# Last output projections of the second attention and of the state space layer, token tile by token tile

## The chip, the cores and the metric

The kernel runs on one core of one Trainium2 chip. The metric is device time in microseconds (us) of one execution; the time of a kernel is the median of its runs. Engines are named as the profile names them: PE (TensorE matmuls), PEld (its weight loads), DVE (VectorE), ACT (ScalarE), POOL (GpSimd), SP (SyncE, which issues most of the DMAs).

## The reference

One sequence of 512 tokens with 1024 features goes through two blocks, all in float32. The first block mixes a gated convolution, a stick-breaking attention and a cross attention to a memory, and ends in a feed-forward layer. The second block is what the change touches:

```
for layer in range(2):
    h = rmsnorm(x, norm_mix[layer])
    mix = attn_layer(h, ...) if layer % 2 == 0 else ssm_layer(h, ...)
    x = x + mix
    h = rmsnorm(x, norm_ffn[layer])
    x = x + conv_ffn(h, ...)        # (silu(causal_dwconv(gate)) * up) @ w_out

attn_layer: ... return concatenate([oa, ob], -1) @ w_out          # 1024 x 1024
ssm_layer:  ... y = rmsnorm of groups of 512 features (yg)
            return y @ w_out                                     # 2048 x 1024
```

The last projection of `attn_layer` takes the 512 features of the heads of kind a (rows 0 to 511 of its `w_out`); the last one of `ssm_layer` takes the 512 features of group 3 (rows 1536 to 2047).

## The kernel before

**Precision by halves.** Every float32 product is made of three fast matmuls (`mm3`): both operands are split into a high part (rounded to fp32r) and a low part (the rest), and high x high, high x low and low x high are accumulated in one PSUM bank. So an operand is ready only when ACT has cast its high part and DVE has subtracted to get the low part. Weights come from HBM into two raw buffers, and go through chunks of 128 x 512 (`whi` by ACT, `wlo` by DVE), nine of which there is room for (`WB`). Activations go through `Feat.put` (L431), which casts (`hh`, `oTh`, `yTh`) and subtracts (`hl`, `oTl`, `yTl`).

**Jobs.** The program is a list of jobs, each a block of weights with a generator `run` that records PE's matmuls. `run_jobs` (L355) records one job after the other; at each `yield` it splits further weight chunks, as far as there is room, and lets other tasks take a step: attention units, state space units, norms. Those tasks sit in a heap ordered by the planner's own clock `now`; `until(...)` lets tasks run until what the job needs has been recorded. The result is one fixed order of instructions on each engine, and each engine works strictly through its own.

**The places in question.** `jobB` is a projection from features to tokens: for each of four token tiles of 128 tokens it accumulates over its weight chunks into one bank (`gb` in the profile), 3 matmuls of 128 x 512 for each of 4 chunks, so 12 for a tile and half. It gives 512 of the 1024 output features; the two halves of the features are two jobs, half 0 for all four tiles and then half 1 for all four. `residual` adds the bank to the residual stream `x` on DVE and, when it is the last such sum, calls the hook of the next norm (`normer`). The hook records for that tile and half: ACT squares the row and sums it (`junk`), and later PE transposes the tile (`tr`), DVE multiplies by the gain (`xg`), ACT casts (`hh`) and DVE subtracts (`hl`). When both halves of a tile are there, the row's scale follows (`rs`).

In the state space layer, `outp(3, True)` is the last projection. Its `pre` waits until all four token tiles of group 3 are recorded (`(g, 3) in S`), where each tile is: PE products `y1` and `y2`, on DVE a join of four rows (`y`, `yo`, `y`, `y`), a square on ACT (`yj`), a power on POOL (`yr`), a scaling on DVE, four transposes on PE (`yT`), and the cast and the difference (`yTh`, `yTl`). In the second attention, the last two jobs use the heads of kind a (`oT`), whose tiles come from a pipeline of units that is still running.

After either place comes a convolutional feed-forward layer. Its first job (`jobA` with `between`) takes features 0 to 511 of all tokens for both of its feature tiles, then features 512 to 1023; `between` then makes a row of all tokens' scales (`R`), which the gated convolution (`fg`, `fy` on DVE) needs.

Of the kernel before, what the change touches and what calls it, by code (L numbers as in the profile page):

```python
# [19 lines left out]
NT = 4  # L20
# [36 lines left out]
class Job:  # L57
    def __init__(self, pieces, nk, nc, run, pre=None):
        self.pieces = pieces
        self.nk = nk  # L60
        self.nc = nc
        self.run = run
        self.pre = pre
        self.speed = 0.6
        self.source = None
        self.after = None
        self.prefetch = None
        self.ahead = None


@with_exitstack
def kernel(ctx: ExitStack, tc: tile.TileContext, ins: dict, out: bass.AP, parts=(1, 2, 3, 4, 5)):
# [59 lines left out]
    def spawn(gen, delay=0.0):  # L132
        count[0] += 1
        heapq.heappush(tasks, (now[0] + delay, count[0], gen))

    def step():

        ready, n, gen = heapq.heappop(tasks)
        now[0] = max(now[0], ready)
        outer, done[0] = done[0], 0.0  # L140
        try:
            d = next(gen)
        except StopIteration:
            done[0] = outer
            return
        d, lag = d if isinstance(d, tuple) else (d or 0.0, LAG)
        heapq.heappush(tasks, (max(now[0] + d, done[0] + lag), n, gen))
        done[0] = outer
# [10 lines left out]
    quota = [2]  # L159
# [3 lines left out]
    def room(tag, n=1):  # L163

        for k, v in freed.items():
            live[k] -= sum(t <= now[0] for t in v)
            freed[k] = [t for t in v if t > now[0]]
        if tag == "g":
            return live["g"] + live["t"] + n <= BANKS
        return live["t"] + n <= BANKS - max(quota[0], live["g"])  # L170

    def bank(tag, nm="p"):

        while not room(tag):
            soon = [t for k in ("g", "t") for t in freed[k]]
            if tag == "g" and soon:
                now[0] = min(soon)
            else:
                until(lambda: room(tag))
        live[tag] += 1  # L180
        return pp.tile([128, 512], F32, tag="ps", name=nm, bufs=BANKS)

    def rel(tag):
        freed[tag].append(max(done[0], now[0]))

    def hand_over():

        live["g"] -= 1
        live["t"] += 1
# [51 lines left out]
    def pump():  # L241
        while tasks and tasks[0][0] <= now[0]:
            step()

    def drain():
        while tasks:
            step()

    def until(ready):

        limit = now[0] + 500.0
        while not ready():
            if tasks:
                step()
            else:
                now[0] += 0.1
            assert now[0] < limit
# [5 lines left out]
    class Flow:  # L263
# [19 lines left out]
        def run(self, units):  # L283

            while units:
                while self.count - self.at[-1] >= self.cap:
                    yield 0.3
                spawn(self.stages(self.count, units.pop(0)))
                self.count += 1
                yield self.every  # L290


    jobs = []
    raws = {}
    split = {}
# [38 lines left out]
    def split_lo():  # L334
        while late:
            late.pop(0)()
# [18 lines left out]
    def run_jobs():  # L355
        chunks = [(i, c) for i, j in enumerate(jobs) for c in range(max(1, j.nk * j.nc // 512))]
        st = {"n": 0, "used": 0}

        def more(limit, upto=None):
            while limit > 0 and st["n"] < len(chunks):  # L360
                i, c = chunks[st["n"]]
                if upto is not None and i > upto:
                    return
                if upto is None and st["used"] - freed_chunks[0] >= WB:
                    return
                split_lo()
                split_hi(i, c)
                st["n"] += 1
                st["used"] += 1
                limit -= 1  # L370

        for i, j in enumerate(jobs):
            if j.pre is not None:
                j.pre()
            more(99, i)
            if late and chunks[st["n"] - 1][0] == i:
                split_lo()
            sp_ = 0.5
            for _ in j.run(W(i)):
                split_lo()  # L380
                sp_ += j.speed
                if sp_ >= 1:
                    more(1)
                    sp_ -= 1
                pump()
            st["used"] -= len(split.pop(i))
            freed_chunks[0] = 0
        drain()

    def mm3(ps, sh, sl, mh, ml, first, last):  # L390
        pe.matmul(ps, lhsT=sh, rhs=mh, start=first, stop=False)
        pe.matmul(ps, lhsT=sh, rhs=ml, start=False, stop=False)
        pe.matmul(ps, lhsT=sl, rhs=mh, start=False, stop=last)

    class Feat:
# [25 lines left out]
        def ready(self, k, a, b):  # L421
            return all((k, t) in self.got for t in range(a, b, 128))
# [84 lines left out]
    def jobB(wap, r0, nk, c0, X, k0, state, first, last, evac, ntt=NT, width=512, pre=None):  # L507

        def run(w):
            x = X()  # L510
            quota[0] = ntt if first and not last else 2
            for tt in range(ntt):
                if first:
                    state[tt] = bank("g", "gb")
                ps = state[tt][:, 0:width]
                for k in range(nk):
                    wh, wl = w.get(k, 0, width)
                    xh, xl = x.rd(k0 + k, tt * 128, tt * 128 + 128)
                    mm3(ps, xh, xl, wh, wl, first and k == 0, last and k == nk - 1)
                    if k % 2 and k + 1 < nk:  # L520
                        yield
                if last:
                    hand_over()
                    if not evac(tt, ps):
                        rel("t")
                yield

        jobs.append(Job([(0, width, wap[r0:r0 + nk * 128, c0:c0 + width])], nk, width, run, pre))
        if ntt < NT:
            jobs[-1].speed = 1  # L530

    def projB(wap, r0, nk, c0, X, evac, ntt=NT, pre=None, k0=0, cut=None, mid=None):
        state = {}
        n = 0
        for m in cut or [4] * (nk // 4):
            jobB(wap, r0 + n * 128, m, c0, X, k0 + n, state, n == 0, n + m == nk, evac, ntt, 512,
                 pre if n == 0 else mid)
            n += m

# [13 lines left out]
    def scaled_add(ps, scale, tt, half):  # L555

        xa = x_half(tt, half)
        dve.scalar_tensor_tensor(out=xa, in0=ps, scalar=scale[:, tt:tt + 1], in1=xa, op0=ALU.mult, op1=ALU.add)
# [182 lines left out]
    hooks = {}  # L741
# [4 lines left out]
    def x_half(tt, h):  # L746
        return x_ap(tt)[:, h * 512:(h + 1) * 512]
# [5 lines left out]
    def x_done(tt, h):  # L753

        hooks["x"](tt, h)
# [68 lines left out]
    def residual(c, last=True, scale=None):  # L824

        def evac(tt, ps):
            xa = x_half(tt, c)
            if scale:
                scaled_add(ps, scale(), tt, c)
            else:  # L830
                dve.tensor_add(xa, ps, xa)
            if last:
                x_done(tt, c)
        return evac
# [4 lines left out]
    def first_block():  # L839
# [140 lines left out]
        for half in range(2):  # L980
            projB(ins["w_mem_kv"], 0, KD, half * 512, lambda: M["m"], k_evac(half), ntt=2)
        for half in range(2):
            projB(ins["w_mem_kv"], 0, KD, D + half * 512, lambda: M["m"], v_evac(half), ntt=2)
# [328 lines left out]
    def attn(G):  # L1312
        w = ins["attn_w_in_2"]
        S = {}
# [178 lines left out]
        X = lambda: G["h"]  # L1493
# [23 lines left out]
        wo = ins["attn_w_out_2"]  # L1517
        O = lambda: oT["o"]
        for half in range(2):
            jobB(wo, 512, 4, half * 512, O, 4, {}, True, True, residual(half, False), pre=va_end)  # L1520
        for half in range(2):
            jobB(wo, 0, 4, half * 512, O, 0, {}, True, True, residual(half),
                 pre=(lambda: hooks.update(x=hooks["next2"])) if half == 0 else None)

# [73 lines left out]
    def ssm(G):  # L1600
        w = ins["ssm_w_in_2"]
        wo = ins["ssm_w_out_2"]
        X = lambda: G["h"]
        S = {}
# [288 lines left out]

        def outp(g, last):
            def pre():
                until(lambda: (g, 3) in S)
                if last:
                    hooks.update(x=hooks["next4"])
            for half in range(2):
                projB(wo, g * 512, 4, half * 512, lambda: S["yT", g], residual(half, last),  # L1900
                      pre=pre if half == 0 else None)

        group(0)
        for g in range(1, 4):
            group(g)
            outp(g - 1, False)
        outp(3, True)


# [110 lines left out]
```

## Time and profile before

| | |
|---|---|
| median of 3 runs | 2476.68 us (2473.72 to 2478.02) |
| profiled execution, its own time | 2474.39 us |
| span of that execution in the trace | 2472.7 us, 30712 instructions |
| PE busy | 2432.4 us (98%) |
| DVE busy | 1527.4 us (62%) |
| ACT busy | 1113.9 us (45%) |
| POOL busy | 215.0 us (9%) |
| granted TensorE clock, mean | 0.998 |

The span is the time from the first to the last instruction; 1.7 us lie around it. Matmuls overlap: one of 128 x 512 has a duration of 0.39 us, but the next starts 0.23 us after it. So PE's busy share does not tell how much of its time is lost; gaps between starts do. In the timeline a bracket at a row's end gives the idle time of the engine just before it and the engine and tile that ended it.

### The profile page before, as it was taken

What the parts mean: (1) busy time and instruction counts of PE and PEld (TensorE: products, weight loads), DVE (VectorE), ACT (ScalarE), POOL (GpSimd) and SP (SyncE); (2) the same over time, 40 slices, a digit from 0 to 9 for tenths busy, and PEclk for the clock granted to TensorE, in tenths of its full rate; (3) what the DMA queues carried; (4) which work ended last, traced back from release to release, by engine and by line L of the source; (5) the groups of instructions that cost most, each with busy time, mean ns of one, the idle gap of its engine ahead of it and who ended that gap; (6) DMA issues with size and microseconds to landing.
All of it is one profiled execution on the core that took longest, in us unless ns stands there. A gap on an engine that the chain in (4) does not pass through costs nothing.

```text
span 2472.7 us, 30712 instructions
## 1 busy us (share of the span) xinstructions
PE 2432.4 (98%) x11556; PEld 1975.4 (80%) x11556; DVE 1527.4 (62%) x2808; ACT 1113.9 (45%) x2406; POOL 215.0 (9%) x279
## 2 busy tenths in 40 slices
PE   8999999999999999999998999999999999999999
PEld 6877877788888888888776888888778887888887
DVE  6436466653434566656756666776698687667674
ACT  6545444432333445545666333333565635433332
POOL 1102011101110011102100000000000000001010
PEclk9999999999999999999999999999999999999999
DMA  5323332333323565622221354442432431345442
GB/s 208 103 59 95 111 100 80 88 109 111 99 89 119 153 163 144 120 91 82 68 87 35 104 143 120 131 107 80 118 107 77 124 115 60 97 142 119 137 111 77
DMA packets 218533, 264.78 MB, mean 107 GB/s; under 512 B 7024, under 2 KB 157936, under 8 KB 218384
## 3 DMA queue, kind: packets, MB, share of 16 engines
q1 hardware_dynamic: 198848, 222.83, 27.8%
q0 software_dynamic: 15232, 29.36, 7.4%
q10 hardware_dynamic: 4304, 10.62, 1.5%
q8 instruction: 91, 1.49, 0.3%
q14 instruction: 58, 0.48, 0.1%
HBM read 254.33 MB, written 4.26 MB: 105 GB/s over the span
## 4 chain that ended last, share of the span: by engine, by line
PE 87%; DVE 6%; issue 4%; ACT 1%; DMA 1%; POOL 0%; ACTq 0%; SPq 0%; POOLq 0%; DVEq 0%
PE ga L87 47%; PE gb L87 21%; PE gw L87 11%; PE y L87 1%; PE as L87 1%; DVE wlo L120 1%; DVE fy L120 1%; PE o L87 1%; PE tr L92 1%; PE aT L92 1%; PE z L87 1%; PE ao L87 1%; PE ap L92 1%; DVE ae L120 0%; DVE y L120 0%
## 5 line engine op out<-in xcount | busy, mean ns | idle before, releaser
L87 PE MATMUL ga<-hh,whi 128*128 128x512 f32 x1672 | 661.4, 396 | 0.0
L87 PE MATMUL ga<-hh,wlo 128*128 128x512 f32 x1672 | 651.8, 390 | 0.3 <-DVE wlo L120 0.2
L87 PE MATMUL ga<-hl,whi 128*128 128x512 f32 x1672 | 651.3, 390 | 0.0
L120 DVE TENSOR_TENSOR wlo<-raw,whi 128x512 fp32r<-128x512 f32 x701 | 479.3, 704 | 227.6 <-ACT whi L120 226.5
L120 ACT CAST whi<-raw 128x512 fp32r<-128x512 f32 x701 | 412.8, 617 | 156.8 <-PE ga L87 62.5
L87 PEld LDWEIGHTS ga<-hh,wlo 128*128 128x128 f32 x1672 | 313.2, 187 | 67.7 <-DVE wlo L120 1.2
L87 PEld LDWEIGHTS ga<-hh,whi 128*128 128x128 f32 x1672 | 313.4, 187 | 66.3 <-issue 3.0
L87 PEld LDWEIGHTS ga<-hl,whi 128*128 128x128 f32 x1672 | 313.6, 188 | 64.9 <-issue 1.7
L87 PE MATMUL gb<-whi,hh 128*128 128x512 f32 (+1 forms) x416 | 171.6, 412 | 0.0
L87 PE MATMUL gb<-wlo,hh 128*128 128x512 f32 (+1 forms) x416 | 159.3, 383 | 2.3 <-DVE wlo L120 2.2
L87 PE MATMUL gb<-whi,hl 128*128 128x512 f32 (+1 forms) x416 | 159.8, 384 | 0.0
L120 DVE TENSOR_TENSOR wlo<-b,whi 128x512 fp32r<-128x512 f32 x196 | 131.2, 686 | 36.9 <-ACT whi L120 36.9
L120 ACT ACTIVATE fy<-fy,cols 128x512 f32<-128x512 f32 x60 | 43.5, 726 | 202.1 <-DVE fy L120 200.4
L120 ACT CAST whi<-b 128x512 fp32r<-128x512 f32 x196 | 114.1, 616 | 15.6 <-PE gw L87 11.2
L120 DVE SCALAR_TENSOR_TENSOR x<-gw,rsp,x 128x512 f32<-128x512 f32 x98 | 70.0, 750 | 69.3 <-PE gw L87 69.2
L120 DVE SCALAR_TENSOR_TENSOR fy<-fg,cols,fy 128x510 f32<-128x510 f32 (+1 forms) x136 | 102.1, 751 | 4.8
L120 DVE TENSOR_TENSOR fg<-ga,R 128x512 f32<-128x512 f32 x68 | 46.9, 690 | 78.6 <-PE ga L87 67.2
L87 PEld LDWEIGHTS gb<-wlo,hh 128*128 128x128 f32 x416 | 78.6, 189 | 17.6 <-DVE wlo L120 3.7
L87 PEld LDWEIGHTS gb<-whi,hl 128*128 128x128 f32 x416 | 78.2, 188 | 16.0
L87 PEld LDWEIGHTS gb<-whi,hh 128*128 128x128 f32 x416 | 78.4, 188 | 14.6 <-issue 1.7
L655 POOL DMA_DIRECT2D b<-in_ffn_w_out_dram x32 | 38.5, 1205 | 507.6 <-DVE wlo L120 503.6
L87 PE MATMUL gw<-whi,fss 128*128 128x512 f32 x256 | 81.4, 389 | 0.0
(316 smaller groups left out, 3958.7 us busy)
## 6 DMA issues: line engine op xcount, KB each, us to landing
raw<-in_ffn_w_in_dram SPq DMA_DIRECT2D x44, 1024.0 KB, 5.1
raw<-in_w_in_dram SPq DMA_DIRECT2D x32, 1024.0 KB, 5.0
raw<-in_w_up_dram SPq DMA_DIRECT2D x16, 1024.0 KB, 5.4
b<-in_ffn_w_out_dram POOLq DMA_DIRECT2D x32, 512.0 KB, 5.7
raw<-in_ssm_w_in_dram SPq DMA_DIRECT2D x16, 1024.0 KB, 5.3
b<-in_w_down_dram POOLq DMA_DIRECT2D x24, 512.0 KB, 6.0
b<-in_ffn_w_out_dram SPq DMA_DIRECT2D x12, 1024.0 KB, 7.6
b<-in_w_down_dram SPq DMA_DIRECT2D x9, 1024.0 KB, 7.7
```

The lines of the kernel that those rows point to most:

```text
L87: nc.tensor.matmul(o, lhsT=lhsT, rhs=rhs, **kw)
L92: nc.tensor.transpose(o, i, idn)
L120: return fn(*args, **kw)
L655: nc.gpsimd.dma_start(out=r3(R[nm][:, a * 512:(c + 1) * 512], c + 1 - a), in_=dram(i, j, a, c + 1), accum_op=ALU.add)
```

## The change

Both halves of the last projection become one loop: for each token tile first half 0, then half 1. A new function `projC` makes two jobs; the first loads and splits the chunks of half 0 and records no matmul, and is kept (`keep`), the second records the matmuls of both. A weight chunk is given free at its use in the last token tile. In the state space layer the wait ahead of the projection is now for tile 0 of group 3 alone.

```diff
@@ class Job
+        self.keep = False
@@ run_jobs
+            if j.keep:
+                continue
             st["used"] -= len(split.pop(i))
+            if i and jobs[i - 1].keep:
+                st["used"] -= len(split.pop(i - 1))
             freed_chunks[0] = 0
@@
+    def projC(wap, r0, nk, X, evac, pre=None):
+
+        def run(w):
+            ws = (W(w.i - 1), w)
+            x = X()
+            quota[0] = 2
+            for tt in range(NT):
+                for half in range(2):
+                    ps = bank("g", "gb")
+                    for k in range(nk):
+                        wh, wl = ws[half].get(k, 0, 512)
+                        xh, xl = x.rd(k, tt * 128, tt * 128 + 128)
+                        mm3(ps, xh, xl, wh, wl, k == 0, k == nk - 1)
+                        if tt == NT - 1:
+                            w.done()
+                        if k % 2 and k + 1 < nk:
+                            yield
+                    hand_over()
+                    evac(half)(tt, ps)
+                    rel("t")
+                    yield
+
+        for half in range(2):
+            jobs.append(Job([(0, 512, wap[r0:r0 + nk * 128, half * 512:(half + 1) * 512])], nk, 512,
+                            run if half else lambda w: (), None if half else pre))
+        jobs[-2].keep = True
@@ attn
-        for half in range(2):
-            jobB(wo, 0, 4, half * 512, O, 0, {}, True, True, residual(half),
-                 pre=(lambda: hooks.update(x=hooks["next2"])) if half == 0 else None)
+        projC(wo, 0, 4, O, residual, lambda: hooks.update(x=hooks["next2"]))
@@ ssm, outp
-                until(lambda: (g, 3) in S)
+                until(lambda: (g, 0 if last else 3) in S)
                 if last:
                     hooks.update(x=hooks["next4"])
+            if last:
+                projC(wo, g * 512, 4, lambda: S["yT", g], residual, pre)
+                return
```

The order of instructions differs at these two places and in the few microseconds after each; elsewhere it is the same, but for source lines and buffer numbers. Three pieces of it follow, all from the state space layer. In the names, `yTh_18143` and `yTl_18144` are the high and low part of group 3's features, `whi_0` to `whi_3` with their `wlo` the four chunks of a half, and `x_6529` holds tiles 0 and 1 of the residual stream, `x_6530` tiles 2 and 3.

PE, at the end of group 2's projection, before:

```order
L87 MATMUL gb<-wlo_3_17972,yTh_17372 128x512
L87 MATMUL gb<-whi_3_17971,yTl_17373 128x512
L87 MATMUL y_18162<-xdt,m 128x64 x8
L87 MATMUL y_18171<-stt,bc 128x512
L92 MATMUL yT<-ident,y 128x128 x12
L87 MATMUL gb<-whi_0_17987,yTh_18143 128x512
L87 MATMUL gb<-wlo_0_17988,yTh_18143 128x512
L87 MATMUL gb<-whi_0_17987,yTl_18144 128x512
```

and now, where tile 0 passes into tile 1:

```order
L88 MATMUL gb<-whi_3_18170,yTh_18143 128x512
L88 MATMUL gb<-wlo_3_18171,yTh_18143 128x512
L88 MATMUL gb<-whi_3_18170,yTl_18144 128x512
L93 MATMUL tr<-ident,x_6529 128x128 x4
L93 MATMUL yT<-ident,y 128x128 x4
L88 MATMUL gb<-whi_0_17987,yTh_18143 128x512
L88 MATMUL gb<-wlo_0_17988,yTh_18143 128x512
L88 MATMUL gb<-whi_0_17987,yTl_18144 128x512
```

The transposes of the tiles 1, 2 and 3 of `yT` stood in one piece ahead of the projection; now tile 0's 24 matmuls stand ahead of them, tile 3's `y1` and `y2` between those, and the transpose of the `x` that the three rows on top have just completed stands directly behind them.

DVE, from the difference of tile 1 to that of tile 3, before:

```order
L120 TENSOR_TENSOR yTl_18144<-yT,yTh_18143 128x4x128
L120 SCALAR_TENSOR_TENSOR y<-y,yr,nw 128x512
L120 TENSOR_SCALAR yr<-yms 128x1
L120 SCALAR_TENSOR_TENSOR y<-y,yr,nw 128x512
L120 TENSOR_TENSOR yTl_18144<-yT,yTh_18143 128x4x128
L120 TENSOR_TENSOR x_6529<-gb,x_6529 128x512
L120 TENSOR_TENSOR wlo_1_18220<-raw_17985,whi_1_18219 128x512
L120 TENSOR_TENSOR yTl_18144<-yT,yTh_18143 128x4x128
```

and now, from the sum of tile 0's half 1 to the difference of tile 1:

```order
L121 TENSOR_TENSOR x_6529<-gb,x_6529 128x512
L121 TENSOR_TENSOR y<-y_18205,y 128x512
L121 TENSOR_TENSOR yo<-y_18214,tok 128x512
L121 TENSOR_TENSOR y<-y,yo 128x512
L121 TENSOR_TENSOR y<-y,sz 128x512
L121 TENSOR_SCALAR yr<-yms 128x1
L121 TENSOR_TENSOR xg<-tr,cols 128x512
L121 TENSOR_SCALAR rs<-ms 128x1
L121 TENSOR_TENSOR hl_18222<-xg,hh_18221 128x4x128
L121 TENSOR_TENSOR yTl_18144<-yT,yTh_18143 128x4x128
```

The join of tile 3 (`y`, `yo`, `y`, `y`) and the norm's rows of tile 0 now stand between the sum of `x` and the difference of tile 1.

PE, at the passage to the feed-forward layer, before (`ga` is its first job):

```order
L87 MATMUL ga<-hh_18251,whi_1_18333 128x512
L87 MATMUL ga<-hl_18252,whi_1_18333 128x512
L87 MATMUL ga<-hh_18251,wlo_1_18334 128x512
L92 MATMUL tr<-ident,x_6530 128x128 x4
L87 MATMUL ga<-hh_18251,whi_0_18296 128x512
L87 MATMUL ga<-hl_18252,whi_0_18296 128x512
```

and now:

```order
L88 MATMUL gb<-whi_3_18170,yTh_18143 128x512
L88 MATMUL gb<-wlo_3_18171,yTh_18143 128x512
L88 MATMUL gb<-whi_3_18170,yTl_18144 128x512
L93 MATMUL tr<-ident,x_6530 128x128 x4
L88 MATMUL ga<-hh_18221,whi_0_18183 128x512
L88 MATMUL ga<-hl_18222,whi_0_18183 128x512
```

The transpose of the last tile's half 1 stood behind 12 matmuls of the next layer; now it stands directly behind the matmuls that complete it, and ahead of all of `ga`.

## Rows read from the trace of the kernel before

**Rows 1.** The page, chain that ended last, shares by engine.

```profile
PE 87%; DVE 6%; issue 4%; ACT 1%; DMA 1%; POOL 0%; ACTq 0%; SPq 0%; POOLq 0%; DVEq 0%
```

**Rows 2.** PE's timeline, state space layer (start us, us, engine line op out<-in).

```profile
2079.43 0.39 PE L87 MATMUL gb<-whi,yTl 128*128 128x512 f32 x1
2079.66 1.89 PE L87 MATMUL y<-xdt,m 128*128 128x64 f32 x16
...
2084.89 1.08 PE L92 MATMUL yT<-ident,y 128*128 128x128 f32 x4 [2.42 <-DVE y L120]
2088.99 1.12 PE L92 MATMUL yT<-ident,y 128*128 128x128 f32 x4 [3.02 <-DVE y L120]
2090.54 1.11 PE L92 MATMUL yT<-ident,y 128*128 128x128 f32 x4 [0.43 <-DVE y L120]
2091.30 0.78 PE L87 MATMUL gb<-whi,yTh 128*128 128x512 f32 x1
...
2095.02 0.40 PE L87 MATMUL gb<-whi,yTh 128*128 128x512 f32 x1
...
2097.10 0.60 PE L92 MATMUL tr<-ident,x 128*128 128x128 f32 x4
```

**Rows 3.** DVE's timeline, state space layer.

```profile
2079.86 0.69 DVE L120 TENSOR_TENSOR x<-gb,x 128x512 f32<-128x512 f32 x1 [1.22 <-PE gb L87]
2080.47 0.68 DVE L120 TENSOR_TENSOR y<-y,y 128x512 f32<-128x512 f32 x1
...
2083.12 0.15 DVE L120 TENSOR_SCALAR yr<-yms 128x1 f32<-128x1 f32 x1
2083.19 0.68 DVE L120 TENSOR_TENSOR yTl<-yT,yTh 128x512 fp32r<-128x512 f32 x1
2084.00 0.75 DVE L120 SCALAR_TENSOR_TENSOR y<-y,yr,nw 128x512 f32<-128x512 f32 x1
2084.66 0.68 DVE L120 TENSOR_TENSOR y<-y,y 128x512 f32<-128x512 f32 x1
```

**Rows 4.** PE's timeline, second attention, waits for tiles of its heads.

```profile
1327.71 0.50 PE L87 MATMUL gb<-whi,oTl 128*128 128x512 f32 x1 [1.72 <-DVE oTl L120]
...
1333.47 0.50 PE L87 MATMUL gb<-whi,oTh 128*128 128x512 f32 x1 [1.01 <-ACT oTh L120]
...
1334.71 0.50 PE L87 MATMUL gb<-whi,oTl 128*128 128x512 f32 x1 [0.51 <-DVE oTl L120]
...
1342.55 0.50 PE L87 MATMUL gb<-whi,oTl 128*128 128x512 f32 x1 [0.33 <-DVE oTl L120]
```

**Rows 5.** Stretches: length, busy PE, PEld, DVE, ACT, POOL, granted clock, DMA, GB/s.

```profile
1325.00:1350.00 25.00, 20.03 (x142) 12.88 (x142) 13.18 (x49) 13.91 (x36) 0.00 (x0) 1.00 0.13 43
...
2075.00:2084.00 9.00, 7.47 (x48) 5.82 (x46) 7.58 (x15) 2.03 (x5) 0.55 (x1) 1.00 0.37 117
2084.50:2094.50 10.00, 6.16 (x20) 4.72 (x21) 5.75 (x11) 3.00 (x6) 1.10 (x2) 0.50 0.01 2
```

**Rows 6.** PE's timeline, passage to the feed-forward layer after the state space layer.

```profile
2117.87 0.39 PE L87 MATMUL gb<-whi,yTl 128*128 128x512 f32 x1
2118.10 0.39 PE L87 MATMUL ga<-hh,whi 128*128 128x512 f32 x1
...
2126.75 1.05 PE L87 MATMUL R<-dg,onesf 128*128 128x128 f32 x8
...
2135.26 0.50 PE L87 MATMUL ga<-hh,wlo 128*128 128x512 f32 x1 [0.19 <-DVE wlo L120]
```

**Rows 7.** ACT's timeline, state space layer.

```profile
2099.85 0.63 ACT L120 ACTIVATE junk<-x 128x512 f32<-128x512 f32 x1 [1.98 <-DVE x L120]
...
2100.48 0.60 ACT L120 CAST hh<-xg 128x512 fp32r<-128x512 f32 x1
2100.99 0.61 ACT L120 CAST whi<-raw 128x512 fp32r<-128x512 f32 x1
```

**Rows 8.** The chain in order of time, same passage (start us, us, what).

```profile
2097.26 0.44 PE tr L92 x4
```

## The prediction

> **What bounds the kernel now.** I read the page's chain first, then PE's timeline at the two places, the timelines of DVE and ACT beside them, and the granted clock by stretches. The chain is PE for 87% of the span, DVE for 6% [rows 1]: PE is always the engine to keep fed, and what the change is worth is the time that PE loses, at these two places, to waits and to a low clock. The reader is to see in [rows 2] that after the last matmul of group 2 PE has only tile 3's products and three groups of transposes left, each of which waits for a chain on DVE. In [rows 3] DVE works through that chain almost without a gap: it is the bound there. [rows 4] show the same thing, milder, where the second attention's last tiles arrive.
>
> **What PE loses before.** In the state space layer the three waits are 2.42 + 3.02 + 0.43 = 5.87 us [rows 2]. The granted clock in that stretch is 0.50, that is 1.2 instead of 2.4 GHz [rows 5]. So three groups of transposes take 1.08 to 1.12 us where one at the full clock takes 0.60 [rows 2]: 1.5 us. From the start of the first projection matmul at 2091.30 to that at 2095.02 lie nine intervals [rows 2], 3.72 us against 9 x 0.23 = 2.07 (0.23 is the step from 2117.87 to 2118.10 [rows 6]): 1.65 us. In all 9.0 us. In the second attention the waits for tiles 2 and 3 that stand in [rows 4] sum to 1.72 + 1.01 + 0.51 + 0.33 = 3.57 us; two shorter ones behind them, for tile 3 alone, stay with the change. All the change can remove is 12.6 us.
>
> **What it moves.** No matmul, cast or sum is added or dropped: 192 projection matmuls, 16 transposes of `x` (groups of four) and all of the tiles' work stay. DMAs stay too; only the next job's weights are asked for a little earlier, from buffers that are free. What changes is who stands behind whom. I follow PE through the new order with the durations of the rows. Building blocks: a matmul's result is there 0.39 - 0.23 = 0.16 us after the next could start, and DVE takes it up 0.04 us later (2079.43 + 0.39 = 2079.82 to 2079.86, [rows 2, 3]); a row of 128 x 512 takes DVE 0.69 us, or 0.60 to the next one's start [rows 3]; `junk` holds ACT for 0.63 us and a cast for 0.51 [rows 7]; four transposes hold PE for 0.44 us [rows 8]. PE starts on tile 0 at 2079.66, where `y1` stood before.
>
> - (a) Tile 0, half 0: the third matmul needs `yTl` of tile 0. DVE's order up to that row is unchanged, so it ends at 2083.19 + 0.68 = 2083.87 [rows 3]. PE has done two matmuls by 2080.12: a wait of 3.8.
> - (b) Behind tile 0's half 1 stands the transpose of that same `x`. It waits for the matmul's tail and DVE's sum: 0.16 + 0.04 + 0.69 + 0.04 = 0.93.
> - (c) Tile 1 needs `yTh`, ahead of which ACT has `junk` of that `x` and a cast: 0.04 + 0.63 + 0.51 + 0.59 + 0.04 = 1.81 behind the sum. PE fills 0.88 with two groups of transposes: 0.93.
> - (d) Its third matmul needs `yTl`. Behind the sum DVE has tile 3's join of four rows (2.65, from 2080.47 to 2083.12 [rows 3]), then `yr` 0.07, `xg` 0.60, `rs` as short as `yr`, `hl` 0.60, `yTl` 0.68: 4.67 from the start of the join, which is 0.09 ahead of the sum's end, so 4.58. PE has spent 0.88 + 0.93 + two matmuls of 0.23 = 2.27: 2.3.
> - (e) The next transpose of a completed `x` has one group of `yT` ahead of it: 0.93 - 0.44 = 0.5.
> - (f) Tile 2's `yTh`, as (c), but with one group of transposes to fill: 1.81 - 0.44 = 1.4.
> - (g) Tile 2's `yTl` behind `xg`, `hl` and a scaling of 0.66 (2084.00 to 2084.66 [rows 3]): 0.04 + 0.63 + 0.51 + 0.04 = 1.22 until the cast for `hl` is there, then 0.60 + 0.66 + 0.68 = 3.16, less PE's 0.44 + 1.37 + 0.46: 0.9.
> - (h) Tile 3's `yTl` stands behind the sum of tile 2's half 1: 0.16 + 0.04 + 0.60 + 0.68 + 0.04 = 1.5, less two matmuls: 1.1.
> - (i) The transpose of the last `x`, as (b): 0.93.
> - (j) `ga` needs `hh` of tile 3's half 0, which ACT has behind `junk` and a weight cast: 1.81 - 0.44 = 1.4.
> - (k) It needs `hl` too, and DVE has two weight rows and an `xg` ahead of it: 0.6 + 0.6 + 0.08 until the second weight cast is there, then 0.60 + 0.60 + 0.68 = 3.16, less 0.44 + 1.4 + 0.23 on PE: 1.1.
>
> The sum of (a) to (k) is 15.3 us. Before, `ga` followed its predecessor without a gap (2117.87 to 2118.10 [rows 6]), because half 0 had been complete for eleven microseconds.
>
> (l) While both halves are kept, eight of nine chunks are taken, so the next layer's weights are prepared later: behind the two groups of gated convolution rows DVE converts chunk 2 where before it converted chunk 3. PE meets it six matmuls earlier: 6 x 0.23 = 1.4 us more than the 0.19 us seen at 2135.26 [rows 6]. This happens at both places, so 2.8.
>
> **The second attention.** (a) to (h) have no counterpart there, since the units of the attention give PE other work between; the 3.57 us go. (i), (j) and (k) come, 3.4 us, by the same order of rows: together -0.1.
>
> **The clock.** How often it falls the trace only bounds. In the stretch of [rows 2, 5], where 5.9 us of waits lie close together, it was at 1.00 until the first of them and then at 0.50; in the second attention, with the waits of [rows 4] and 5 us without a matmul in 25, it stayed at 1.00 [rows 5]. So a cluster of waits counts as a fall here where it is nearer to the first stretch than to the second: (a), 3.8 in one piece; (b) to (d), 4.2 us with 1.3 of work between; (i) to (k), 3.4 with 0.7, at both places. I count none for (f) and (g), 2.3 us, or (h). A fall costs 1.65 us on the matmuls behind it, as measured above: four are 6.6. Bounds: no fall at all, 0, and six falls, 9.9.
>
> **The sum.** 15.3 - 9.0 (state space) - 0.1 (attention) + 2.8 (weights) + 6.6 (clock) = +15.6 us on the profiled execution's 2474.4: 2490.0. That execution lies 2.3 us under the median of the runs and inside their range; I take 2490.
>
> **Rivals.**
>
> *The filling works (faster).* PE now has 24 matmuls of tile 0, 5.5 us, to do while DVE joins tiles 2 and 3; if those cover the chain and no new wait forms, all of the 12.6 us goes: 2461.8. For it speaks that PE's waits of [rows 2] come from exactly that chain. Against it: DVE is the bound there and gets more to do, the sums and norm rows of tile 0, ahead of the chain's end. It decides at (d): `yTl` of tile 1 would have to be ready 2.3 us sooner, and (b), (f), (j) would each need other work behind the last matmul. Chance 0.10.
>
> *A wash.* Some waits shrink because DVE and ACT reach the rows sooner than the durations say, with falls of the clock at (a) alone: added waits of about 12 instead of 15.3 + 3.4 = 18.7, 1.4 for the weights, 1.65 for the clock: 12 + 1.4 + 1.65 - 12.6 = +2.5, 2476.9. Chance 0.13.
>
> *The waits, but a clock that holds.* All of (a) to (l), no fall: 15.6 - 6.6 = +9.0, 2483.4. For it, the waits of [rows 4] and the granted clock of 1.00 there [rows 5]; against it, (a) alone is longer than any wait in [rows 2], where the clock did fall. Chance 0.20.
>
> *A clock that swings.* Every cluster of waits lowers it, (f) to (h) and the second attention's tiles too: six falls, 9.0 + 9.9 = +18.9, 2493.3. The Trainium skill, TensorE: Matmul & The Clock Gate, section "A second HAM failure mode: psum-queue depth-cycling", says that a PE that pauses briefly but often between groups of matmuls can go back and forth between the two clock levels, and pays for each change. By that rule all six clusters count; the waits of [rows 4], with a clock of 1.00 [rows 5], do not bear it out. Chance 0.17.
>
> My forecast has 0.40.
>
> **Range and chances.** A difference of 0.2%, 5 us, is about what a measurement of this kernel can tell from none. From below: no fall, and waits 15% shorter than worked out (0.15 x 18.7 = 2.8), 2480.6. From above: six falls, the profiled execution's 2.3 us to the median, and 2 us for waits that grow: 2497.6. Between these ends lie forecast and the two rivals on the clock, 0.77; to leave out no more than 2 in 10 the range takes in the wash at 2476.9 as well. So 2476.5 to 2497.5; the likeliest case alone spans 2485 to 2495, for three to five falls and 15% on the waits. Faster by over 0.2%: 0.10, the first rival. Within 0.2%: 0.13, the wash. Slower: 0.77.
>
> **What would show it.** Right: in the state space layer PE waits for `yTl` some 3.8 us at the start of tile 0, then at most 0.5 us less than (c) and (d) at tile 1; transposes of `x` that wait for DVE `x`; `ga` that waits for ACT `hh`, then DVE `hl`, at two places; a wait for `wlo` of over 1 us a few microseconds after `R`; and granted clocks of 0.50 at three stretches of the state space tail and one at the attention's end. From the end of group 2's projection to `R`, 2079.66 to 2126.75 before [rows 2, 6], so 47.1 us, it should take 47.1 + 6.3 + 3 x 1.65 = 58.4. Wrong: waits named for other engines, `ga` that follows without a gap, or a single fall of the clock.

## The result, and the profile after

| | before | after |
|---|---|---|
| median of the runs shown | 2476.16 us (2473.72 to 2478.02, 4 runs) | 2488.61 us (2488.21 to 2492.45, 4 runs) |
| profiled execution, span | 2472.7 us | 2486.8 us |
| PE busy | 2432.4 us | 2436.7 us |
| granted TensorE clock, mean | 0.998 | 0.997 |

The change makes the kernel 12.4 us slower by the medians and 14.1 us by the two spans; the ratio is 1.0055, with an interval of 1.004 to 1.007. The chain's shares by engine [rows 1] are the same after, PE 87% and DVE 6%.

PE's timeline in the state space layer after the change, to be read beside [rows 2, 6]; the start of the first transposes of group 3 stands on top, `R` and the wait for the next weights at the bottom:

```profile
2079.67 0.60 PE L93 MATMUL yT<-ident,y 128*128 128x128 f32 x4
...
2085.75 0.80 PE L88 MATMUL gb<-whi,yTl 128*128 128x512 f32 x1 [3.63 <-DVE yTl L121]
...
2097.76 0.66 PE L93 MATMUL tr<-ident,x 128*128 128x128 f32 x4 [0.79 <-DVE x L121]
...
2099.53 0.50 PE L88 MATMUL gb<-whi,yTh 128*128 128x512 f32 x1 [0.67 <-ACT yTh L121]
...
2102.39 0.80 PE L88 MATMUL gb<-whi,yTl 128*128 128x512 f32 x1 [2.13 <-DVE yTl L121]
...
2110.39 0.66 PE L93 MATMUL tr<-ident,x 128*128 128x128 f32 x4 [0.35 <-DVE yr L121]
...
2112.19 0.50 PE L88 MATMUL gb<-whi,yTh 128*128 128x512 f32 x1 [1.15 <-ACT yTh L121]
...
2113.70 0.50 PE L88 MATMUL gb<-whi,yTl 128*128 128x512 f32 x1 [0.78 <-DVE yTl L121]
...
2121.26 0.50 PE L88 MATMUL gb<-whi,yTl 128*128 128x512 f32 x1 [0.93 <-DVE yTl L121]
...
2128.27 0.66 PE L93 MATMUL tr<-ident,x 128*128 128x128 f32 x4 [0.79 <-DVE x L121]
...
2130.05 0.51 PE L88 MATMUL ga<-hh,whi 128*128 128x512 f32 x1 [1.12 <-ACT hh L121]
2131.46 0.50 PE L88 MATMUL ga<-hl,whi 128*128 128x512 f32 x1 [0.90 <-DVE hl L121]
...
2139.50 1.05 PE L88 MATMUL R<-dg,onesf 128*128 128x128 f32 x8
...
2148.01 0.50 PE L88 MATMUL ga<-hh,wlo 128*128 128x512 f32 x1 [1.54 <-DVE wlo L121]
```

Three waits, all for `y`, have become eleven, for `yTh`, `yTl`, `x`, `hh` and `hl`, in the order (a) to (k) of the prediction. What DVE does during the first shows why it is long; DVE's timeline after, to be read beside [rows 3]:

```profile
2081.69 0.69 DVE L121 TENSOR_TENSOR x<-gb,x 128x512 f32<-128x512 f32 x1 [1.22 <-PE gb L88]
2082.30 0.68 DVE L121 TENSOR_TENSOR y<-y,y 128x512 f32<-128x512 f32 x1
2082.90 0.68 DVE L121 TENSOR_TENSOR yo<-y,tok 128x512 f32<-128x512 f32 x1
2083.61 0.69 DVE L121 TENSOR_TENSOR y<-y,yo 128x512 f32<-128x512 f32 x1
2084.34 0.69 DVE L121 TENSOR_TENSOR y<-y,sz 128x512 f32<-128x512 f32 x1
2084.95 0.15 DVE L121 TENSOR_SCALAR yr<-yms 128x1 f32<-128x1 f32 x1
2085.01 0.68 DVE L121 TENSOR_TENSOR yTl<-yT,yTh 128x512 fp32r<-128x512 f32 x1
```

`yTl` of tile 0, the last row, stands behind group 2's last sum (`x`), for which DVE itself waits 1.22 us, and behind a tile's join (`y`, `yo`, `y`, `y`). The matmul that needs it starts as it ends (2085.01 + 0.68 = 2085.69, and the matmul at 2085.75).

In the second attention the four waits of [rows 4] are gone. What is left, and what is new at the passage to the feed-forward layer:

```profile
1350.81 0.50 PE L88 MATMUL gb<-whi,oTh 128*128 128x512 f32 x1 [0.84 <-ACT oTh L121]
...
1353.16 0.50 PE L88 MATMUL gb<-whi,oTh 128*128 128x512 f32 x1 [0.36 <-ACT oTh L121]
...
1358.11 0.66 PE L93 MATMUL tr<-ident,x 128*128 128x128 f32 x4 [0.78 <-DVE x L121]
1359.95 0.50 PE L88 MATMUL ga<-hh,whi 128*128 128x512 f32 x1 [1.19 <-ACT hh L121]
1361.36 0.76 PE L88 MATMUL ga<-hl,whi 128*128 128x512 f32 x1 [0.90 <-DVE hl L121]
...
1379.49 0.50 PE L88 MATMUL ga<-hh,wlo 128*128 128x512 f32 x1 [1.49 <-DVE wlo L121]
```

The granted clock by stretches after (columns as in [rows 5]): low behind (k) in the attention, behind (a) and behind (d), and at 1.00 behind (k) in the state space layer:

```profile
1361.00:1365.00 4.00, 3.64 (x9) 2.89 (x10) 2.42 (x8) 0.88 (x2) 0.93 (x1) 0.57 0.82 266
2085.00:2092.00 7.00, 6.25 (x15) 4.96 (x16) 3.79 (x8) 0.85 (x3) 0.55 (x1) 0.51 0.45 150
2092.00:2102.00 10.00, 6.80 (x41) 4.92 (x39) 6.27 (x12) 2.22 (x6) 1.33 (x2) 1.00 0.00 0
2102.00:2106.00 4.00, 3.61 (x10) 2.86 (x10) 0.34 (x1) 0.00 (x0) 0.14 (x1) 0.57 0.00 0
2120.00:2136.00 16.00, 12.27 (x57) 9.24 (x56) 10.49 (x21) 6.94 (x15) 1.47 (x2) 1.00 0.20 67
```

### The profile page after: what moved, and what is told of

Its sections match the earlier page's. It is cut to its first block, busy times and chain, and to the rows that moved or that the text cites. A ratio compares the mean times of both kernels' runs of the same rounds, so it can differ in the third digit from the quotient of the medians.

```text
span 2486.8 us, 30712 instructions
## 1 busy us (share of the span) xinstructions
PE 2436.7 (98%) x11556; PEld 1977.8 (80%) x11556; DVE 1528.0 (61%) x2812; ACT 1112.3 (45%) x2402; POOL 215.5 (9%) x279
## 3 DMA queue, kind: packets, MB, share of 16 engines
q8 instruction: 91, 1.49, 0.2%
## 4 chain that ended last, share of the span: by engine, by line
PE 87%; DVE 6%; issue 4%; ACT 1%; DMA 1%; POOL 0%; ACTq 0%; SPq 0%; POOLq 0%; DVEq 0%
PE ga L88 47%; PE gb L88 21%; PE gw L88 11%; PE y L88 1%; PE as L88 1%; DVE wlo L121 1%; DVE fy L121 1%; PE o L88 1%; PE tr L93 1%; PE ao L88 1%; PE aT L93 1%; PE z L88 1%; PE ap L93 1%; DVE y L121 0%; PE st L88 0%
## 5 line engine op out<-in xcount | busy, mean ns | idle before, releaser
L121 ACT CAST whi<-b 128x512 fp32r<-128x512 f32 x196 | 114.1, 616 | 15.6 <-PE gw L88 11.2
```

The costliest lines, as they stand in the source:

```text
L121: return fn(*args, **kw)
```

## Experiments

**Theory and rivals.** Theory: each new wait is work that stands behind other work in the strict order of DVE or ACT, and PE meets it because tile-by-tile order leaves no other matmuls in between; a low clock comes on top. Rivals: the chain from matmul to transposed tile is simply that long, whatever is queued; and the clock alone makes the loss. Where an expectation below speaks of theory A and rival or theory B, they are those of its own run.

Two stretches tell where the time went, both from the profiled executions. **Q**, second attention: from the end of PE's wait for `qz` at 1301.35 us before to `R`. **S**, state space layer: from the first `yT` of group 3 to `R`. In kernels that leave a stretch as it was, it repeats within about 0.1 us (Q; in e4 a stray fall of the clock, far from the edit, makes it 1.2 us longer) and 0.5 us (S). PE's timeline before, with the start and end of Q, a wait inside it, and the start of S (its end, `R` at 2126.75, is in [rows 6]):

```profile
1301.35 0.91 PE L87 MATMUL as<-ka,qz 128*128 128x384 f32 x2 [1.08 <-ACT qz L120]
...
1318.26 1.12 PE L87 MATMUL as<-ka,qz 128*128 128x512 f32 x2 [0.62 <-ACT qz L120]
...
1370.78 1.05 PE L87 MATMUL R<-dg,onesf 128*128 128x128 f32 x8
...
2077.84 0.60 PE L92 MATMUL yT<-ident,y 128*128 128x128 f32 x4
```

and Q after:

```profile
1302.26 0.91 PE L88 MATMUL as<-ka,qz 128*128 128x384 f32 x2 [1.07 <-ACT qz L121]
...
1371.04 1.05 PE L88 MATMUL R<-dg,onesf 128*128 128x128 f32 x8
```

| kernel | median us | ratio to before, interval | Q us | S us | wait for `wlo` behind `R` in S |
|---|---|---|---|---|---|
| before | 2476.2 | | 69.43 | 48.91 | 0.19 |
| after | 2488.61 | 1.0055, 1.004 to 1.007 | 68.78 | 59.83 | 1.54 |
| e1 attention alone | 2476.98 | 1.0005, 0.9996 to 1.0013 | 68.79 | 48.39 | 0.18 |
| e2 state space alone | 2487.76 | 1.0047, 1.0035 to 1.006 | 69.47 | 63.15 | 1.55 |
| e3 e2, all tiles awaited | 2483.97 | 1.0031, 1.002 to 1.0043 | 69.46 | 53.89 | 1.55 |
| e4 early start, half by half | 2485.57 | 1.0039, 1.0025 to 1.0053 | 70.60 | 57.30 | 0.18 |
| e6 after, waits filled | 2486.82 | 1.0042, 1.0029 to 1.0055 | 68.82 | 58.82 | 1.54 |
| e7 attention, last tiles by halves | 2472.09 | 0.9984, 0.9975 to 0.9993 | 65.34 | 48.59 | 0.19 |
| e11 e2, put at once | 2483.33 | 1.0031, 1.0019 to 1.0042 | 69.42 | 54.75 | 1.55 |
| e12 e2, sums held | 2481.81 | 1.0023, 1.0014 to 1.0032 | 69.42 | 53.34 | 1.49 |
| e13 e2, last tiles by halves | 2481.63 | 1.0029, 1.0019 to 1.004 | 69.41 | 54.25 | 0.19 |
| e9 e2, all three | 2470.74 | 0.9978, 0.9968 to 0.9987 | 69.45 | 44.35 | 0.18 |
| e10 e7 and e9 | 2466.16 | 0.996, 0.9948 to 0.9973 | 65.34 | 42.84 | 0.18 |

**The two places apart.** e1 takes the state space part of the change back:

```diff
-                until(lambda: (g, 0 if last else 3) in S)
+                until(lambda: (g, 3) in S)
-            if last:
-                projC(wo, g * 512, 4, lambda: S["yT", g], residual, pre)
-                return
```

> Token order in the second attention alone, the state space layer as before. By the waits behind one another: 3.6 us of waits for late tiles go, 2.9 us of new ones come at the passage to the feed-forward layer (transpose for DVE x, ga for ACT hh and DVE hl), 1.4 us for the converted weights and 1.65 us for one fall of the clock: +1.5 to +2.5 us. If the new waits were hidden by other work, or the clock alone made the difference: -3.6 to 0.

e2 takes the attention's part back:

```diff
-        projC(wo, 0, 4, O, residual, lambda: hooks.update(x=hooks["next2"]))
+        for half in range(2):
+            jobB(wo, 0, 4, half * 512, O, 0, {}, True, True, residual(half),
+                 pre=(lambda: hooks.update(x=hooks["next2"])) if half == 0 else None)
```

> Token order and early start in the state space layer alone, the attention as before. By the waits: nearly all of the loss, +10 to +12 us. If the two places shared the loss, +6.

The medians lie 1.1 and 11.9 us above the 2475.84 of before beside them, 13.0 in sum against 12.4 for both: the two losses add up as far as these runs can tell, and nearly all of the loss is in the state space layer. e1 alone came out a little under its +1.5 to +2.5, and its interval holds 1, so its time does not tell it from its rival; its trace does, for the waits of 0.79, 1.18 and 0.90 us stand at the passage.

**The two steps in the state space layer apart.** e3 is e2 with the wait for all four tiles; e4 is e2 with the start at tile 0 kept and the halves in the old order:

```diff
# e3
-                until(lambda: (g, 0 if last else 3) in S)
+                until(lambda: (g, 3) in S)
# e4
-            if last:
-                projC(wo, g * 512, 4, lambda: S["yT", g], residual, pre)
-                return
```

> Token order in the state space layer, but the projection starts only when all four tiles of group 3 are recorded; attention as before. By the waits: the 9.0 us lost before stay, the waits inside tiles 0 to 3 do not arise, those at the passage (2.9 us) and for converted weights (1.4 us) do, perhaps with a second fall of the clock: +4 to +6 us. Rival, that the early start alone does the harm and the token order none: 0 to +1.5.

> Half by half as before in both places, but the state space projection starts as soon as tile 0 is there. By the waits: 3.8 us at tile 0 and waits for ACT yTh and DVE yTl at tiles 1 to 3, about 13 us in place of 9.0 with one or two more falls of the clock, but ga follows without a gap and no wait for converted weights over 0.5 us: +4 to +8 us. Rival, that the early start alone does all the harm: +11. Rival, that filling PE early helps as long as halves stay in order: -3 to -7.

They cost 8.1 and 9.7 us, each more than expected, and 17.8 in sum against 11.9 together: here the steps are not independent. e3 keeps before's 2.42, 3.02 and 0.43 us and adds the passage's waits of 0.79, 1.12 and 0.90, the `wlo` wait, and a fall of the clock at the passage. The expectation's upper end, +6, had allowed for all of these, and the profiled execution of e3, the fastest of its six at 2481.48 us, is 5.6 us above before's median; what makes its median 2.5 us longer than that is not shown. e4 has the wait of 3.63 us, then 1.44, 0.68 and 1.84 for tile 1, 0.56 and 0.78 for tile 2, 0.35 for a sum `x` and 1.15 for tile 3, with the clock low behind the first and the fourth of these, and no wait at the passage and only 0.18 us for `wlo`. So the passage's waits and (l) come from the token order, and (a) and the waits for the tiles 1 to 3 come with the early start; e3 still pays before's three waits for `y`, of which e4 keeps one.

**The clock.** e6 is the changed kernel with matmuls that nothing reads, in the bank that the next real one starts afresh:

```diff
                     ps = bank("g", "gb")
+                    if half == 0 and tt < len(fill):
+                        for _ in range(fill[tt]):
+                            nc.tensor.matmul(ps, lhsT=x.rd(0, 0, 128)[0], rhs=ws[0].get(0, 0, 512)[0], start=True, stop=True)
...
-                projC(wo, g * 512, 4, lambda: S["yT", g], residual, pre)
+                projC(wo, g * 512, 4, lambda: S["yT", g], residual, pre, (14, 10))
```

> The changed kernel with 14 matmuls that nothing reads ahead of the last projection's first tile in the state space layer and 10 ahead of its second, where TensorE otherwise stands still (3.63 and then 0.79 and 0.67 us ahead of tile 0, 2.13 us ahead of tile 1). They are real work on the chip and leave nothing in the output. Theory A, that the lowered clock there is a cost of its own: the granted clock of the two stretches rises from 0.51 and 0.57 towards 1.00, which gives back some 3.1 and 1.6 us, so 3 to 5 us below the changed kernel's 2488.6, which is a ratio of about 1.003 to 1.004 to the kernel before. Theory B, that the time there is set by the chain of VectorE and ScalarE that yields the transposed tiles: what TensorE does meanwhile is of no matter, and the time stays within 1 us of 2488.6 (ratio 1.005), with shorter matmuls and correspondingly longer waits behind them.

PE's timeline of e6, and its stretches:

```profile
2080.68 0.60 PE L93 MATMUL yT<-ident,y 128*128 128x128 f32 x4
...
2082.51 3.36 PE L556 MATMUL gb<-whi,yTh 128*128 128x512 f32 x14
...
2086.76 0.50 PE L88 MATMUL gb<-whi,yTl 128*128 128x512 f32 x1 [0.45 <-DVE yTl L121]
...
2107.11 0.66 PE L93 MATMUL tr<-ident,x 128*128 128x128 f32 x4 [0.35 <-DVE yr L121]
```

```profile
2085.00:2092.00 7.00, 6.55 (x36) 5.34 (x35) 4.76 (x9) 1.96 (x5) 0.55 (x1) 1.00 0.32 105
...
2108.00:2114.00 6.00, 4.31 (x11) 3.14 (x12) 2.49 (x5) 1.38 (x3) 0.55 (x1) 0.72 0.01 3
2128.00:2136.00 8.00, 6.71 (x21) 5.12 (x22) 3.85 (x10) 1.99 (x4) 0.93 (x1) 0.79 0.40 131
```

The filling does what theory A says where it is put: the clock stays at 1.00, and from the first `yT` to the wait (e) it takes 2107.11 - 2080.68 = 26.43 us against 2110.39 - 2079.67 = 30.72. But PE still starts on `yTl` of tile 0 only as DVE ends it, as B says: 6.08 us behind the first `yT` in both kernels (2086.76 - 2080.68, 2085.75 - 2079.67). And 3.3 of the 4.3 us are lost again behind (e) (to `R`, 32.39 us against 29.11), where the clock now falls twice, behind waits of the same length that had left it at 1.00 in the changed kernel. The median is 1.8 us below the changed kernel's, and the intervals overlap: the total is between A and B, and a lasting gain from filling is not shown.

**Order of the last tiles, attention.** e7 puts tiles 2 and 3 half by half into the attention's part; the loop runs over a list:

```diff
-            for tt in range(NT):
-                for half in range(2):
+            for n, (tt, half) in enumerate(order):
...
-        projC(wo, 0, 4, O, residual, lambda: hooks.update(x=hooks["next2"]))
+        projC(wo, 0, 4, O, residual, ((0, 0), (0, 1), (1, 0), (1, 1), (2, 0), (3, 0), (2, 1), (3, 1)), 0, lambda: hooks.update(x=hooks["next2"]))
```

> The attention's part of the change alone, with one more step: the order of the eight tile halves is tile 0 first and second half, tile 1 first and second half, then tiles 2 and 3 first half, tiles 2 and 3 second half. The state space layer is as before. Theory A (the new waits of the change at the passage come from tile 3's two evictions, statistics and transposes all falling together at the very end): with tile 2's and tile 3's first halves out of the way the waits of 0.79, 1.19 and 0.90 us there go back to the 0.44 and 0.19 of before or to nothing, while the waits of 1.72, 1.01, 0.51 and 0.33 us for the attention's late tiles are as short as in the change. Gain 2 to 3.5 us on before, ratio 0.9986 to 0.9992. Rival B (the waits come from the token order as a whole, whose last halves follow each other however tiles 2 and 3 are arranged): waits of about 2.9 us in sum stay there and the ratio is about 1.0005, as it was with the attention's part alone.

PE's timeline of e7 at the passage, and the stretch:

```profile
1360.03 0.39 PE L88 MATMUL ga<-hh,whi 128*128 128x512 f32 x1
1360.25 0.42 PE L88 MATMUL ga<-hl,whi 128*128 128x512 f32 x1
```

```profile
1355.00:1372.00 17.00, 17.00 (x86) 14.07 (x85) 10.37 (x22) 8.11 (x18) 1.48 (x2) 1.00 0.20 63
```

`ga` follows without a gap, the clock stays at 1.00, and Q falls by 4.1 us against before. Three waits for `oTh`, of 1.09, 0.90 and 0.36 us, are left in Q, where the change has two, of 0.84 and 0.36. The kernel is 4.2 us faster than before, a little over the range expected by theory A; B is out.

**The state space layer.** e9 is e2 with three steps: the same list of halves; the sums and norm rows of both halves of tile 0 put behind the matmuls of tile 1's first half; and tile 0's cast and difference recorded at once and not as a task that waits its turn:

```diff
+                held.append((tt, half, ps))
+                if n < hold:
+                    yield
+                    continue
+                while held:
+                    t, h, p = held.pop(0)
+                    evac(h)(t, p)
...
-                    spawn(S["yT", g].put(0, r3(ps, 4), tt * 128, tt * 128 + 128, "t"))
+                    put = S["yT", g].put(0, r3(ps, 4), tt * 128, tt * 128 + 128, "t")
+                    if g == 3 and tt in (0,):
+                        for _ in put:
+                            pass
+                    else:
+                        spawn(put)
```

> The state space layer's part of the change alone, with three more steps. The order of the halves is that of the run before this one; the addition of the result to the residual and the norm's sums of tile 0's two halves are put behind the matmuls of the next half; and tile 0's transposed halves are written to memory as soon as they are there, ahead of what VectorE has queued. Theory A (each long wait of the change is VectorE or ScalarE doing, in their strict order, work that could wait while TensorE stands for work that is queued behind it): the 3.63 us ahead of tile 0 shrinks below 1.5, the 2.13 ahead of tile 1 stays, and the 0.35, 1.15, 0.78, 0.93 of the later tiles and the 0.79, 1.12, 0.90 of the passage go mostly. Gain 3 to 8 us on before, ratio 0.9968 to 0.9988. Rival B (the wait is the length of the chain itself, from the group's last matmul to a transposed tile, whatever is queued): waits of 3 us or more stay ahead of tile 0, and the ratio is 1.000 to 1.003.

DVE's timeline of e9, then all of PE's waits between the first `yT` and `R`:

```profile
2080.49 0.69 DVE L121 TENSOR_TENSOR yTl<-yT,yTh 128x512 fp32r<-128x512 f32 x1 [0.45 <-ACT yTh L121]
2081.26 0.69 DVE L121 TENSOR_TENSOR x<-gb,x 128x512 f32<-128x512 f32 x1
```

```profile
2085.25 0.50 PE L88 MATMUL gb<-wlo,yTh 128*128 128x512 f32 x1 [0.39 <-DVE wlo L121]
...
2091.69 0.63 PE L93 MATMUL yT<-ident,y 128*128 128x128 f32 x4 [1.67 <-DVE y L121]
...
2092.79 1.12 PE L93 MATMUL yT<-ident,y 128*128 128x128 f32 x4 [0.47 <-DVE yr L121]
```

With `yTl` ahead of the sum, not behind it and a join, the wait of 3.63 us is gone altogether; where e2 has eleven waits three are left, and S is 4.6 us shorter than before. The 2.13 us for tile 1's `yTl`, which theory A had staying, are gone too; PE waits 1.67 us for that tile's `y` instead. The kernel is 5.5 us faster than before, with 17.0 us between it and e2: theory A, and the length of the chain was not the cause of the 3.63 us.

**The three steps one at a time**, each alone on e2: e11 only records tile 0's `put` at once, e12 only holds the sums, e13 only uses the list of halves.

> The state space layer's part of the change alone (which was 11.9 us above before), with one of the three steps that together turned it into a gain of 5.5 us: tile 0's transposed halves are written as soon as they are there. Theory A (the 3.63 us ahead of tile 0 are VectorE's queue and nothing else): that wait falls under 1.5 us with its lowered clock, which is worth 2.2 us of waiting and up to 3.1 us of clock; the token order's waits at tiles 1 to 3 and at the passage stay in sum. 3 to 6 us below the part alone, so 6 to 9 us above before, ratio 1.0024 to 1.0036. Rival B (one step alone gives nothing, since TensorE only comes earlier to the next wait): within 1.5 us of 2487.8, ratio 1.0042 to 1.0054, and the wait for tile 1's transposes grows by as much as tile 0's falls.

> The state space layer's part of the change alone, with the second of the three steps: the additions to the residual and the norm's sums of tile 0's two halves are put behind the matmuls of the next half. Theory A (the 0.78 us ahead of the norm's transposes and the 2.12 us for tile 1's transposed tile come from VectorE and ScalarE doing tile 0's residual first): these two go or shrink below 1 us, with the lowered clock behind them (1.6 us), the 3.63 ahead of tile 0 and the passage's waits of 0.79, 1.12, 0.90 stay. 3 to 6 us below the part alone, so 6 to 9 above before, ratio 1.0024 to 1.0036. Rival B (the time moves to the wait behind it): within 1.5 us of 2487.8, ratio 1.0042 to 1.0054.

> The state space layer's part of the change alone, with the third of the three steps: tiles 2 and 3 half by half. Theory A (as it was in the attention, where this step was worth 5.3 us): the passage's 0.79, 1.12, 0.90 us go, while what lies before tile 2 stays as in the part alone; tile 3's wait for its transposes may move up, as its first half now comes before tile 2's second. 2 to 5 us below the part alone, so 7 to 10 above before, ratio 1.0028 to 1.004. Rival B (with the late tiles 2 and 3 still due, an order that comes to tile 3 earlier waits there for what it saves at the passage): within 1.5 us of 2487.8, ratio 1.0042 to 1.0054.

The medians are 4.4, 6.0 and 6.1 us below e2's, 16.5 in sum against 17.0 together (by the ratios 1.6 + 2.4 + 1.8 = 5.8 thousandths against 6.9, each with an interval of about 1 to either side). e11: the 3.63 us are gone, but tile 1's waits grow from 0.68 + 2.12 to 2.72 (`y`) + 0.90 (`yTh`) + 0.29 (`yTl`), so 1.1 of the 3.6 us come back, a part of what its rival B said; the waits (e) to (h) of the later tiles go too, which neither theory had. e12: 0.78 and 2.12 us go, 3.63 and the passage stay; of the waits (e) to (h) one of 1.24 us is left, which had not been expected either. e13: the passage's three waits, (h) and (l) go, and two of 0.35 and 0.57 us come for tile 3; it gains 1.1 us more than expected. No single step gets back to before; each removes the waits that it was meant for.

**Both places.** e10 is e7 and e9 in one kernel, with no further edit.

> The two runs before this one together: the attention's last projection with the last two tiles half by half, and the state space layer's likewise, with tile 0's sums put back and its transposed halves written at once. If the two places are independent of each other, as they were in the change (its parts alone gave +1.1 and +11.9 us, together +12.5), the time is the sum of the two gains: 5 to 11 us below the kernel before, ratio 0.9956 to 0.998. If they share a cost (a clock that stays up or falls in both), the sum is missed by more than 1.5 us.

Its median is 10.1 us below before, against 4.2 + 5.5 = 9.7: the places add up again. These stretches of e10, which take in the tails of both places, show a clock at 1.00:

```profile
1355.00:1372.00 17.00, 17.00 (x87) 14.04 (x85) 10.40 (x21) 7.96 (x18) 1.48 (x2) 1.00 0.19 63
2078.00:2091.00 13.00, 10.46 (x55) 7.83 (x54) 11.34 (x22) 3.98 (x9) 2.34 (x3) 1.00 0.27 86
2091.00:2120.00 29.00, 29.00 (x151) 24.17 (x151) 20.41 (x40) 14.28 (x33) 2.97 (x4) 1.00 0.12 37
```

So an early start can beat the kernel before, once the orders of DVE and ACT follow it and the last two tiles go half by half.

## Why the prediction was right

The forecast was 2490 us and +15.6 on the profiled execution; 2488.61 and +14.1 were measured.

**(a) to (k), right in kind and size.** Each wait stands where it was forecast, for the tile that was named but for (e), which the profile names for `yr`: the sum `x` ends 0.06 us ahead of PE's start there (2109.64 + 0.69), and in e4 a wait of the same 0.35 us is named for `x`. The brackets are 0.1 to 0.3 us shorter than the working, because a bracket begins at the matmul's modelled end, 0.16 us after the next could have started: (a) has 3.63 us in its bracket and 3.79 from start to start. The Trainium skill, Perfetto Trace Analysis, "Tensor Engine Instruction (MATMUL, LD_WEIGHTS)", says that a matmul's end in a profile is an estimate, not a measurement. No run here shows that by itself; the 0.39 us of duration beside the 0.23 from start to start are in keeping with it. Taken from start to start, less the step of the work between, as the prediction worked:

| | (a) | (b) | (c) | (d) | (e) | (f) | (g) | (h) | (i) | (j) | (k) | sum |
|---|---|---|---|---|---|---|---|---|---|---|---|---|
| predicted | 3.8 | 0.93 | 0.93 | 2.3 | 0.5 | 1.4 | 0.9 | 1.1 | 0.93 | 1.4 | 1.1 | 15.3 |
| measured | 3.79 | 0.94 | 0.84 | 2.29 | 0.51 | 1.36 | 0.94 | 1.09 | 0.95 | 1.34 | 1.18 | 15.2 |

From the end of group 2 to `R` it takes 2139.50 - 2081.49 = 58.0 us; 58.4 were forecast, 47.1 it was.

**(l), right.** Forecast 1.4 us at each place; 1.54 - 0.19 = 1.35 and, against a gap of 0.12 us before (1378.71 + 0.39 to 1379.22), 1.49 - 0.12 = 1.37. That it comes from the chunks kept is borne out by e4 and e13, where half 0's chunks come free earlier and 0.18 and 0.19 us are left.

**The second attention, mis-sized.** The term was -0.1 us without the clock. New waits of 3.53 us from start to start (3.4 forecast) and 1.68 us lost to a low clock stand in Q, and yet Q is 0.65 us shorter: so 3.53 + 1.68 + 0.65 = 5.9 us went, not 3.57. The forecast summed brackets, which leave out 0.16 us each, and missed a wait of 0.62 us for `qz` at 1318.26, which also goes; with these, 5.0 us are accounted for, and the other 0.9 are not. The term should have been -2.3.

**The clock, right in size by luck.** Four falls at 1.65 us, 6.6 in all, were counted. The profiled execution has three: behind (a), where the 14 intervals from 2085.75 to 2091.89 lose 2.92 us, nearly twice the price; behind (d), 1.54; in the attention, 1.68. That is 6.1 us. Behind (i) to (k) in the state space layer there was none, against the forecast, but e2 has one there, and one behind (f) and (g) too, with the same waits within 0.02 us; its stretches:

```profile
2112.00:2116.00 4.00, 3.35 (x8) 2.68 (x9) 0.71 (x2) 0.00 (x0) 0.55 (x1) 0.60 0.00 0
2132.00:2136.00 4.00, 3.99 (x12) 3.20 (x13) 2.06 (x7) 0.53 (x2) 0.93 (x1) 0.66 0.79 259
```

So the rule by which falls were counted fails: in the state space layer the same order with the same waits gave two falls in one execution and four in another. There the clock of e2, and not that of the changed kernel's profiled execution, goes as the rival with the swinging clock had it. One of the four runs of the changed kernel took 2492.45 us at a mean clock of 0.995, near that rival's 2493.3; it has no trace, so how often the clock fell in it is not shown.

**The sum.** Q -0.65, (l) 1.37 + 1.35, the state space layer 58.0 - 47.1 = 10.9: 13.0. The other 1.1 us of the 14.1 lie outside these places, 0.91 of them ahead of Q; the medians differ by 12.4. So the forecast had 2.2 us too much in the second attention and 0.5 in the clock, and 1.1 us that it did not count came from elsewhere: that 14.1 is so near to 15.6 is in part luck, while the waits (a) to (l), which decide the direction, were right one by one.

**The rivals.** The filling that works, given 0.10, failed where it was said to, at (d), and at (a) too; e9 and e10 show what it lacked, an order on DVE and ACT in which tile 0's and tile 1's features do not stand behind sums and norm rows, and work of another half behind the last results. The wash failed: the waits are not shorter. A clock that holds, 2483.4, did not come about; in e6 the clock held as far as (e) and fell twice behind it.

## What to carry to other kernels

In this kernel starting a consumer earlier and in another order paid only once the engines that feed it followed. So walk the producers' strict orders to each row that the consumer will now want first, and look for sums and norms of work already done that stand ahead of it. At a passage between layers, leave some work of another tile behind the last result, since otherwise PE waits for its whole chain of sum, transpose, cast and difference. Take lost time on PE from start to start, and give the clock a range, not a count.

## What was not expected of the hardware

The order of instructions and the lengths of the waits did not settle the granted clock. With the same waits, S was 59.83 us in the changed kernel and 63.15 in e2, with two and four stretches at a low clock. e9 and e10 both have the waits of 1.67 to 1.68 and 0.47 to 0.48 us for `y`: in e9 the clock was low behind them (0.67 over 2091 to 2096 us), in e10 it was 1.00, and S is 44.35 and 42.84 us. Five executions of e2 took 2484.57 to 2490.71 us, the shortest at a mean clock of 0.999 and the longest at 0.996; five of e10, at 0.999 to 1.000, lie within 2.04 us. What decides whether a wait lowers the clock is open.
